# Pools that wait tile by tile, and two pairs of staging tiles for the kept weights, in a two-layer decoder kernel

## The chip, the cores and the metric

The kernel runs on one core of a Trainium2 chip. The metric is the device time of one execution in microseconds (us), as the median of several runs. TensorE is called PE here, VectorE DVE, ScalarE ACT, GpSimd POOL and SyncE SP.

## What is computed

A decoder trunk of two layers on one sequence of 1024 positions with 1024 channels, in float32. Layer 0 mixes by a diagonal state-space model (S5) with a gated output product, layer 1 by stick-breaking attention; each ends with a squared-ReLU MLP of width 4096. Shift, scale and gate of each sub-layer come from a vector c through `ada_w`. Cut to what matters:

```python
for i in range(2):
    sh_a, sc_a, g_a, sh_m, sc_m, g_m = ada_chunks(c, ada_w[i], ada_b[i], 6)
    if i == 0:
        y = s5_mixer(modulate(rms_norm(x, ...), sh_a, sc_a), ...)
        val, gate = split(gelu(y) @ s5_w_glu)
        mix = val * sigmoid(gate)
    else:
        k, v = split(modulate(rms_norm(x, ...), kv_shift, kv_scale) @ w_kv)
        q = modulate(rms_norm(x, ...), sh_a, sc_a) @ sb_w_q
        mix = stick_breaking_attention(norm(q), norm(k), v) @ sb_w_o
    x = x + g_a * mix
    h = modulate(rms_norm(x, ...), sh_m, sc_m)
    x = x + g_m * (square(relu(h @ mlp_w1[i])) @ mlp_w2[i])
```

## The kernel before, in words

**Products.** Every float32 matrix is held as a rounded part and a remainder (`uh` and `ul` for weights, `hi` and `lo` for activations), and `mm3` (L247 to L249) makes three matmuls of one product. A weight unit of 128x1024 is loaded through SP into one of the three `raw` tiles (L208), copied to `uh` by ACT (L214), and DVE makes `ul` by a subtraction (L84; helper lines such as L70, L75, L78, L81, L84 and L93 hold the arithmetic of many places, so the tile names tell which).

**Stages, in us of the profiled execution.** S5 to about 235; the gated product (GLU) to about 400; the MLP of layer 0 to about 1130; the norms of layer 1, then attention from 1145 to 1790; the output projection to 1830; the MLP of layer 1 to the end.

**Side jobs.** Beside GLU and the MLP of layer 0 two kinds of jobs run that prepare later stages. A *gemv* job loads 128 rows of the transposed `ada_w` (512 KB, L173, tile `raw`, through SP, the same three `raw` tiles as the weight units) and reduces them against a row on DVE (L174). A *keep* job works on POOL alone: load 256 KB of `wo`, `wkv` or `wq` into tile `ks` (L227), for `wkv` and `wq` multiply by a scale (L78, `scl`), round into tile `kr` (L232), subtract (L84), and store both to HBM as `kh` and `kl` (L235), so that attention and the output projection later only fetch them (L240). There are 64 keep jobs, 16 for `wo` and 48 for `wkv` and `wq`. `queue` mixes two gemv jobs to one keep job, and `pump`, called from `glu` and from `mid` in the MLP, takes jobs off that list. POOL also adds squares for the norms (L81, tile `f`), which the MLP's norm waits for.

**What sets the order.** S5 has an order written by hand; the rest is put in order by a scheduler when the program is built, and each engine and each DMA queue then issues in that order.

**Tiles and pools.** Pool `adap` has one `ks` and one `kr`, so the next keep load waits until the store of the last one has read `ks`. The class `Inner` gives the tiles `f` (halves of the MLP's hidden activations, work tiles of the norms) in turn from pool "a" (8) and pool "b" (20), and the raw results `ra` and `rb` from "b". A pool opened on bytes of a released pool lets its first instructions wait for every user of what was released. Pools opened late are those of attention (`atp`, `atk`, `atq`, `pz`, `ppt`, `ppo`) and, after it, the pool `x` into which 16 loads bring the residual back from HBM (`x<-xd`, L1611).

```python
raw = adap.tile([P, HN], F32, tag="ks", name=nm("ks"), bufs=1)
hi = adap.tile([P, HN], F32R, tag="kr", name=nm("kr"), bufs=1)
G.dma_start(raw, src[:, cs])
```

Of the kernel before, what the change touches and what calls it, by code (L numbers as in the profile page):

```python
# [8 lines left out]
F32 = mybir.dt.float32  # L9
F32R = mybir.dt.float32r  # L10
# [11 lines left out]
HN = 512  # L22
# [34 lines left out]
def kernel(ctx, tc, A, out):  # L57
# [42 lines left out]
    pools, turns = {}, {}  # L100

    def open_x(i):
        es = ExitStack()
        pools["x"] = es.enter_context(tc.tile_pool(name=f"xp{i}", bufs=16 if i else 1))
        pools["raw"] = es.enter_context(tc.tile_pool(name=f"raw{i}", bufs=3))
        es.callback(pools.pop, "raw")
        turns.clear()
        return es

    def open_ax(i):  # L110
        es = ExitStack()
        pools["ax"] = es.enter_context(tc.tile_pool(name=f"pax{i}", bufs=4 if "pv" in pools else 6, space=PSUM))
        return es

    cnt = [0]
# [13 lines left out]

    def open_pv():  # L130
        es = ExitStack()
        pools["pv"] = es.enter_context(tc.tile_pool(name="ppv", bufs=2, space=PSUM))
        es.callback(pools.pop, "pv")
        return es

# [57 lines left out]
    def queue(jobs, n, others):  # L193
        while jobs or others:
            side.extend(jobs[:n] + others[:1])
            del jobs[:n], others[:1]

    def scale_cols(n, sc0):
        stt(scl[:, 8 * n:8 * n + 8], mod[:, sc0:sc0 + 8], 1.0, gcol[:, 8 * n:8 * n + 8],
            ALU.add, ALU.mult)  # L200
# [15 lines left out]
        return uh, ul  # L216


    kept = {}

    def keep(key, src, c, scale=None):
        if c == 0:
            kept[key] = [dp.tile([P, 1024], F32, name=nm(name)) for name in ("kh", "kl")]
        cs = slice(HN * c, HN * c + HN)
        raw = adap.tile([P, HN], F32, tag="ks", name=nm("ks"), bufs=1)
        hi = adap.tile([P, HN], F32R, tag="kr", name=nm("kr"), bufs=1)
        G.dma_start(raw, src[:, cs])  # L227
        if scale is not None:
            nk = scale.shape[1] // 2
            r3 = raw.rearrange("p (k m) -> p k m", k=nk)  # L230
            mul(r3, r3, scale[:, nk * c:nk * c + nk].unsqueeze(2).broadcast_to([P, nk, HN // nk]), G)
# [25 lines left out]

    def s5(hook):
        es = ExitStack()
        sp = es.enter_context(tc.tile_pool(name="sp", bufs=1))  # L260
        pp = es.enter_context(tc.tile_pool(name="s5ps", bufs=2, space=PSUM))

        cst = sp.tile([P, C_N], F32, name="cst")
        SP.dma_start(cst, A["cst"])
# [70 lines left out]
        dt, mag, th = s("dt"), s("mag"), s("th")  # L335
# [4 lines left out]
        n, r, z = s("e1"), s("e2"), s("e3")  # L340
# [203 lines left out]
        class Block:  # L544
# [165 lines left out]
            pv, vt = None, None  # L710
# [93 lines left out]
    class Norm:  # L804
# [56 lines left out]
    class Inner:  # L861
# [3 lines left out]
            self.n, self.es, self.pools = 0, ExitStack(), {}  # L865

        def open(self, name):
            self.pools[name] = self.es.enter_context(tc.tile_pool(name="fp" + name, bufs=1))

        def tile(self, dt=F32R):  # L870
            a = self.n % 28 < 8
            self.n += 1
            return self.pools["ab"[not a]].tile([P, HN], dt, tag="f", name=nm("f"), bufs=8 if a else 20)

        def raw(self, tag):
            return self.pools["b"].tile([P, HN], F32, tag=tag, name=nm(tag), bufs=2)
# [13 lines left out]
    def mlp(layer, xs, hs, norm, fs, mid=None, done=None):  # L890
        w1, w2 = A["w1"][layer], A["w2"][layer]
        gm = M_GM0 if layer == 0 else M_GM1
        f_tile = fs.tile
        hid, raws = {}, {}
# [7 lines left out]
            mul(r, r, r)  # L902
            return r

        def halves(r):
            hi, lo = f_tile(), f_tile()
            ACT.copy(hi, r)  # L907
            sub(lo, r, hi)
            return hi, lo
# [8 lines left out]
        def enter(j, h, r):  # L918
            raws[j, h] = r
            i = j % 2  # L920
            if (j, h) == (1, 0) or (j, h) == (2, 0):
                hid["B11", i] = halves(raws[i, 0])
            if h == 1 and j >= 2:
                b11, b12, b21, b22 = raws[i, 0], raws[i, 1], raws[j, 0], raws[j, 1]
                hid["B21", i] = halves(b21)
                hid["B22", i] = halves(b22)
                sub(b22, b22, b12)
                hid["T3", i] = halves(b22)
                sub(b12, b12, b11)
                hid["T1", i] = halves(b12)  # L930
                add(b11, b11, b22)
                hid["T2", i] = halves(b11)
                sub(b21, b21, b11)
                hid["T4", i] = halves(b21)

        def blocks(c, op):
            raw = raw_tile()
# [119 lines left out]

    def attention(xn, bias, xd):
        es = ExitStack()
        ap_ = es.enter_context(tc.tile_pool(name="atp", bufs=1))  # L1060
        ak_ = es.enter_context(tc.tile_pool(name="atk", bufs=1))
        aq_ = es.enter_context(tc.tile_pool(name="atq", bufs=1))

        pz = es.enter_context(tc.tile_pool(name="pz", bufs=3, space=PSUM))
        ppt = es.enter_context(tc.tile_pool(name="ppt", bufs=2, space=PSUM))
        ppo = es.enter_context(tc.tile_pool(name="ppo", bufs=1, space=PSUM))
# [382 lines left out]
        return oh, ou[-2:]  # L1449


    pools["un"] = ctx.enter_context(tc.tile_pool(name="unp", bufs=3))
# [4 lines left out]
    rowp = ada_es.enter_context(tc.tile_pool(name="rowp", bufs=1))  # L1457
    silr = rowp.tile([P, D], F32, name="silr")

    def gate(i):  # L1460
# [6 lines left out]
    def hook(i):  # L1467
# [7 lines left out]
        if i == 1:  # L1475
            gate(0)

    ys = s5(hook)
    adap = ada_es.enter_context(tc.tile_pool(name="adap", bufs=1))
    ax_es = open_ax(0)  # L1480
    xs = [[None, None] for _ in range(8)]
    ordered[0] = True
# [3 lines left out]
            SP.dma_start(xs[k][h], A["xT"][k][:, HN * h:HN * h + HN])  # L1486
    ordered[0] = False
    hs = [[None, None] for _ in range(8)]
    fs = Inner()
    fs.open("a")  # L1490
    norm = Norm(norm_tiles(fs), xs, hs, 2, M_SHM0)
    with tc.tile_pool(name="gp", bufs=1) as gp:
        queue(ada_chunk(M_SHM0) + ada_chunk(M_SCM0, lambda: scale_cols(2, M_SCM0)) + ada_chunk(M_GM0), 2,
              [(lambda i=i, c=c: keep(("o", i), A["wo"][i], c)) for i in range(8) for c in range(2)])

        def glu(i, ug, uv, h):
            ps = ps_pv if h == 1 and i <= 5 else ps_mm
# [12 lines left out]
            norm.square(i, h)  # L1510

        for i in range(6):
            ug, uv = first if i == 0 else (load_unit(A["wglu"][8 + i]), load_unit(A["wglu"][i]))
            for h in range(2):
                glu(i, ug, uv, h)
                if i == 0:
                    for c in range(1 + 3 * h, 4 + 4 * h):
                        gate(c)
            if i:
                pump(9)  # L1520
        for h in range(2):
            for i in range(6, 8):
                ug = load_unit(A["wglu"][8 + i])
                uv = load_unit(A["wglu"][i])
                glu(i, ug, uv, h)
            if h == 0:
                norm.rstd(0)
# [83 lines left out]
            SP.dma_start(xs2[k][h], xd[k][h])  # L1611
    fs = Inner()
    ctx.enter_context(fs.es)
    fs.open("a")
    fs.open("b")
    norm2.np_ = norm_tiles(fs)

    def oproj(i, h, mms):
# [114 lines left out]
```

## Time and profile before

| | us |
|---|---|
| median of 3 runs | 2509.57 (2506.57 to 2510.95) |
| profiled execution | 2508.75 |
| its span | 2507.0 |
| PE busy in the span | 2342.5 |
| DVE busy | 1733.1 |
| ACT busy | 941.7 |
| POOL busy | 908.5 |

The profiled execution lies 0.82 us under the median, and 1.75 us of it lie outside the span. PE is the busiest engine, but not in every stage: the time it lacks is spread over S5, GLU, the MLP of layer 0 and the two ends of attention, and each has to be read by itself.

### The profile page before, as it was taken

To read this page: it belongs to the slowest core of one execution; us is meant where nothing else is said; L and a number is where in the kernel's file an instruction comes from. 1 tells how busy PE (TensorE), PEld (TensorE's weight loads), DVE (VectorE), ACT (ScalarE), POOL (GpSimd) and SP (SyncE) were. 2 spreads that over 40 slices of the span, in tenths; PEclk is the share of its full clock that TensorE was granted. 3 is DMA by queue.
4 is the path that set the end of the run, shared out by engine and by line. 5 is a ranking of instruction groups with operands and counts; after the bars stand their busy time and mean duration, and the time that the engine had idled before them with its cause. 6 is when DMAs were issued, how large, how long until landed. Compare 5 with 4: busy or idle time off the path is not lost.

```text
span 2507.0 us, 33262 instructions
## 1 busy us (share of the span) xinstructions
PE 2342.5 (93%) x12536; PEld 1974.6 (79%) x12536; DVE 1733.1 (69%) x2574; ACT 941.7 (38%) x1710; POOL 908.5 (36%) x963
## 2 busy tenths in 40 slices
PE   3888999999999999997899999998999999999998
PEld 2767787878788888886888888886778888888886
DVE  7997547766655655454677877787583767876787
ACT  4753124211222122132566666665351232223221
POOL 4663343244444445223333332343110322342334
PEclk8899999999999999998999999999999999999999
DMA  4325754655655544232111111126721111111112
GB/s 150 88 77 193 259 186 157 213 205 192 204 196 182 193 175 173 94 119 85 59 56 51 56 64 68 62 100 213 248 87 51 34 51 59 59 43 51 56 54 76
DMA packets 105344, 297.08 MB, mean 119 GB/s; under 512 B 13280, under 2 KB 25568, under 8 KB 105184
## 3 DMA queue, kind: packets, MB, share of 16 engines
q1 hardware_dynamic: 87264, 240.42, 27.9%
q0 software_dynamic: 15360, 50.34, 5.6%
q10 hardware_dynamic: 2560, 4.20, 0.8%
q8 instruction: 99, 1.62, 0.3%
q14 instruction: 61, 0.50, 0.1%
HBM read 241.23 MB, written 49.48 MB: 116 GB/s over the span
## 4 chain that ended last, share of the span: by engine, by line
PE 66%; DVE 16%; DMA 9%; issue 4%; ACT 2%; POOL 0%; SPq 0%; DVEq 0%; ACTq 0%; POOLq 0%
PE pm L247 9%; PE pm L248 9%; PE pm L249 9%; PE pm L70 8%; DMA raw<-in_adaT_dram 7%; PE pa L969 3%; PE pa L971 3%; PE pa L970 3%; PE pa L249 3%; PE pa L247 3%; PE pa L248 3%; PE pt L70 3%; DVE sn L1250 3%; PE po L70 2%; PE z L70 2%
## 5 line engine op out<-in xcount | busy, mean ns | idle before, releaser
L247 PE MATMUL pm<-h,uh 128*128 128x512 f32 x1200 | 469.3, 394 | 23.8 <-issue 13.8
L249 PE MATMUL pm<-h,ul 128*128 128x512 f32 x1200 | 469.9, 392 | 4.6 <-DVE ul L84 4.6
L248 PE MATMUL pm<-h,uh 128*128 128x512 f32 x1200 | 471.2, 393 | 1.0 <-DVE h L93 0.9
L214 ACT CAST uh<-raw 128x1024 fp32r<-128x1024 f32 x130 | 136.6, 1051 | 481.8 <-PE pa L248 153.1
L247 PEld LDWEIGHTS pm<-h,uh 128*128 128x128 f32 x1200 | 227.5, 190 | 74.2 <-issue 14.0
L174 DVE CUSTOM_DVE_ANT_0 raw<-raw,silr 128x1024 f32<-128x1024 f32 x119 | 162.1, 1365 | 174.0 <-DMA raw<-in_adaT_dram 160.1
L84 DVE TENSOR_TENSOR ul<-raw,uh 128x1024 fp32r<-128x1024 f32 (+1 forms) x158 | 192.4, 1218 | 124.5 <-ACT uh L214 101.8
L249 PEld LDWEIGHTS pm<-h,ul 128*128 128x128 f32 x1200 | 227.6, 190 | 53.5 <-DVE ul L84 5.9
L248 PEld LDWEIGHTS pm<-h,uh 128*128 128x128 f32 x1200 | 227.6, 190 | 49.5 <-DVE h L93 2.3
L70 PE MATMUL pm<-uh,h 128*128 128x256 f32 x960 | 223.0, 299 | 0.0
L1250 DVE TENSOR_TENSOR_SCAN sn<-sn 128x768 f32<-128x768 f32 (+7 forms) x128 | 180.5, 1416 | 47.3 <-ACT sn L1245 45.9
L81 POOL TENSOR_TENSOR raw<-raw 128x256 f32<-128x256 f32 x28 | 26.0, 927 | 412.3 <-DVE ul L84 412.3
L70 PEld LDWEIGHTS pm<-uh,h 128*128 128x128 f32 x960 | 169.1, 196 | 0.5
L969 PE MATMUL pa<-f,uh 128*128 128x512 f32 x392 | 153.2, 391 | 3.3 <-ACT f L907 2.6
L247 PE MATMUL pa<-f,uh 128*128 128x512 f32 x396 | 154.4, 390 | 0.0
L248 PE MATMUL pa<-f,uh 128*128 128x512 f32 x396 | 154.1, 389 | 0.0
L249 PE MATMUL pa<-f,ul 128*128 128x512 f32 x396 | 153.8, 389 | 0.0
L970 PE MATMUL pa<-f,uh 128*128 128x512 f32 x392 | 153.1, 391 | 0.0
L971 PE MATMUL pa<-f,ul 128*128 128x512 f32 x392 | 145.9, 390 | 0.0
L70 PE MATMUL pm<-ul,h 128*128 128x256 f32 x480 | 137.9, 287 | 0.0
L78 POOL TENSOR_TENSOR sg<-sg,sn 128x512 f32<-128x512 f32 x64 | 92.9, 1452 | 123.5 <-DVE sn L1250 57.4
L78 POOL TENSOR_TENSOR ks<-ks,scl 128x512 f32<-128x512 f32 x48 | 61.2, 1274 | 196.2 <-DMA ks<-in_wkv_dram 96.7
(363 smaller groups left out, 5370.5 us busy)
## 6 DMA issues: line engine op xcount, KB each, us to landing
raw<-in_w_dram SPq DMA_DIRECT2D x140, 512.0 KB, 3.3
raw<-in_adaT_dram SPq DMA_DIRECT2D x96, 512.0 KB, 4.1
uh<-kh SPq DMA_DIRECT2D x40, 512.0 KB, 4.1
ul<-kl SPq DMA_DIRECT2D x40, 512.0 KB, 4.1
kh<-kr POOLq DMA_DIRECT2D x64, 256.0 KB, 2.4
kl<-ks POOLq DMA_DIRECT2D x64, 256.0 KB, 3.1
raw<-in_wT_dram SPq DMA_DIRECT2D x24, 512.0 KB, 4.5
raw<-in_wglu_dram SPq DMA_DIRECT2D x20, 512.0 KB, 4.2
```

The costliest lines, as they stand in the source:

```text
L70: return lambda *a, **k: tc.keep_in_program_order(f(*a, **k))
L78: eng.tensor_tensor(o, a, b, op=ALU.mult)
L84: eng.tensor_tensor(o, a, b, op=ALU.subtract)
L174: V.tensor_tensor_reduce(raw, raw, row, 1.0, 0.0, op0=ALU.mult, op1=ALU.add, accum_out=bcol)
L214: ACT.copy(uh, raw)
L247: T.matmul(ps, uh[:, sl], hi, start=first, stop=False)
L248: T.matmul(ps, uh[:, sl], lo, start=False, stop=False)
L249: T.matmul(ps, ul[:, sl], hi, start=False, stop=last)
L969: T.matmul(p, uh[:, sl], hi, start=(i == 0), stop=False)
L970: T.matmul(p, uh[:, sl], lo, start=False, stop=False)
L971: T.matmul(p, ul[:, sl], hi, start=False, stop=(i == 1))
L1250: V.tensor_tensor_scan(g[:, s0:], g[:, s0:], g[:, s0:], 1.0, op0=ALU.mult, op1=ALU.bypass)
```

## The change

1. All pools that are opened on released bytes are opened with `reuse_waits="tile"`: an instruction on a new tile waits for the users of those old tiles whose bytes it overlays, and not for all users of the old pool.
2. `adap` is gone. `keep` takes its tiles from a new pool "e" of `Inner`: four of its eight tiles, two pairs, of which the first serves the left half of a weight and the second the right half. Successive keep jobs thus use different tiles.
3. `Inner`'s pool "a" has 20 `f` tiles, "e" has 8, and "b" only `ra` and `rb`. In layer 1 the halves (`wide=True`) go round all 28 as before; in layer 0 all `f` tiles go round the 20 of "a".

```diff
+    def tile_pool(name, bufs=1, **k):
+        return tc.tile_pool(name=name, bufs=bufs, reuse_waits="tile", **k)
...
-        pools["x"] = es.enter_context(tc.tile_pool(name=f"xp{i}", bufs=16 if i else 1))
-        pools["raw"] = es.enter_context(tc.tile_pool(name=f"raw{i}", bufs=3))
+        pools["x"] = es.enter_context(tile_pool(f"xp{i}", bufs=16 if i else 1))
+        pools["raw"] = es.enter_context(tile_pool(f"raw{i}", bufs=3))
...
-        raw = adap.tile([P, HN], F32, tag="ks", name=nm("ks"), bufs=1)
-        hi = adap.tile([P, HN], F32R, tag="kr", name=nm("kr"), bufs=1)
+        while len(keeps) < 4:
+            keeps.append(fs0.extra((F32, F32R)[len(keeps) % 2]))
+        raw, hi = keeps[0:2] if c == 0 else keeps[2:4]
...
-        def tile(self, dt=F32R):
-            a = self.n % 28 < 8
-            self.n += 1
-            return self.pools["ab"[not a]].tile([P, HN], dt, tag="f", name=nm("f"), bufs=8 if a else 20)
+        def tile(self, dt=F32R, wide=False):
+            self.n += wide
+            if wide and (self.n - 1) % 28 >= 20:
+                return self.extra(dt)
+            return self.pools["a"].tile([P, HN], dt, tag="f", name=nm("f"), bufs=20)
+
+        def extra(self, dt):
+            return self.pools["e"].tile([P, HN], dt, tag="e", name=nm("e"), bufs=8)
...
-        ap_ = es.enter_context(tc.tile_pool(name="atp", bufs=1))
-        ak_ = es.enter_context(tc.tile_pool(name="atk", bufs=1))
-        aq_ = es.enter_context(tc.tile_pool(name="atq", bufs=1))
+        ap_ = es.enter_context(tile_pool("atp", bufs=1))
+        ak_ = es.enter_context(tile_pool("atk", bufs=1))
+        aq_ = es.enter_context(tile_pool("atq", bufs=1))
...
-    adap = ada_es.enter_context(tc.tile_pool(name="adap", bufs=1))
...
-    fs = Inner()
+    fs = fs0 = Inner()
     fs.open("a")
+    fs.open("e")
```

Both programs have the same number of instructions on every engine. In the rows below a name's number tells tiles of the same kind apart only where it is needed.

**POOL in the MLP of layer 0**, in its steady run of keep jobs on `wkv`; before (a load, L227, stands behind both stores of the job ahead of it):

```order
L227 DMA ks_5373<-in_wkv_dram 128x512
L78 TENSOR_TENSOR ks_5373<-ks_5373,scl 128x512
L232 CAST kr_5374<-ks_5373 128x512
L84 TENSOR_TENSOR ks_5373<-ks_5373,kr_5374 128x512
L235 DMA kh_5295<-kr_5374 128x512
L235 DMA kl_5296<-ks_5373 128x512
L227 DMA ks_5451<-in_wkv_dram 128x512
L78 TENSOR_TENSOR ks_5451<-ks_5451,scl 128x512
L232 CAST kr_5452<-ks_5451 128x512
L84 TENSOR_TENSOR ks_5451<-ks_5451,kr_5452 128x512
```


and now (`e_2492` with `e_2493` is one pair, `e_2494` with `e_2495` the other; the keep load is L231, the rounding L236, the stores L239):

```order
L239 DMA kl_5248<-e_2492 128x512
L78 TENSOR_TENSOR e_2494<-e_2494,scl 128x512
L236 CAST e_2495<-e_2494 128x512
L231 DMA e_2492<-in_wkv_dram 128x512
L84 TENSOR_TENSOR e_2494<-e_2494,e_2495 128x512
L239 DMA kh_5247<-e_2495 128x512
L239 DMA kl_5248<-e_2494 128x512
L78 TENSOR_TENSOR e_2492<-e_2492,scl 128x512
L236 CAST e_2493<-e_2492 128x512
L231 DMA e_2494<-in_wkv_dram 128x512
```


The load of the next job has moved ahead of the subtraction and the two stores of the job in work.

**POOL at the start of GLU**, up to the first sum of squares for the norm (the L81 row); before:

```order
L70 TENSOR_TENSOR h_2119<-xall,h_2118 128x512
L227 DMA ks_2492<-in_wo_dram 128x512
L70 TENSOR_TENSOR h_2182<-xall,h_2181 128x512
L70 TENSOR_TENSOR h_2186<-xall,h_2185 128x512
L232 CAST kr_2493<-ks_2492 128x512
L84 TENSOR_TENSOR ks_2492<-ks_2492,kr_2493 128x512
L235 DMA kh_2490<-kr_2493 128x512
L235 DMA kl_2491<-ks_2492 128x512
L227 DMA ks_2505<-in_wo_dram 128x512
L232 CAST kr_2506<-ks_2505 128x512
L84 TENSOR_TENSOR ks_2505<-ks_2505,kr_2506 128x512
L235 DMA kh_2490<-kr_2506 128x512
L81 TENSOR_TENSOR f_2273<-f_2273,f_2425 128x512
```


and now:

```order
L70 TENSOR_TENSOR h_2119<-xall,h_2118 128x512
L231 DMA e_2492<-in_wo_dram 128x512
L70 TENSOR_TENSOR h_2182<-xall,h_2181 128x512
L70 TENSOR_TENSOR h_2186<-xall,h_2185 128x512
L236 CAST e_2493<-e_2492 128x512
L231 DMA e_2494<-in_wo_dram 128x512
L84 TENSOR_TENSOR e_2492<-e_2492,e_2493 128x512
L239 DMA kh_2490<-e_2493 128x512
L239 DMA kl_2491<-e_2492 128x512
L236 CAST e_2495<-e_2494 128x512
L84 TENSOR_TENSOR e_2494<-e_2494,e_2495 128x512
L239 DMA kh_2490<-e_2495 128x512
L239 DMA kl_2491<-e_2494 128x512
L231 DMA e_2492<-in_wo_dram 128x512
L231 DMA e_2494<-in_wo_dram 128x512
L81 TENSOR_TENSOR f_2273<-f_2273,f_2425 128x512
```


Four keep loads stand ahead of the first sum of squares where two stood.

**SP at the end of attention**, with what each row waits for (semaphores by engine, `DMAHW` for a queue); before:

```order
L240 DMA ul_16359<-kl_2821 128x1024 [waits DMAHW0_49,PE_49]
L1345 DMA xd_1_3530<-kn_16131 128x512 [waits DMAHW1_49,DVE_49]
L1611 DMA x_16371<-xd_0_3525 128x512 [waits DVE_49,DMAHW2_49,PE_49,Pool_49]
L1611 DMA x_16373<-xd_0_3527 128x512 [waits DMAHW3_49]
L1611 DMA x_16375<-xd_0_3529 128x512 [waits DMAHW4_49]
```


and now:

```order
L244 DMA ul_16235<-kl_2813 128x1024 [waits DMAHW0_49,PE_49]
L1353 DMA xd_1_3502<-kn_16007 128x512 [waits DMAHW1_49,DVE_49]
L1619 DMA x_16247<-xd_0_3497 128x512 [waits DMAHW2_49,Activation_49]
L1619 DMA x_16249<-xd_0_3499 128x512 [waits DMAHW3_49]
L1619 DMA x_16251<-xd_0_3501 128x512 [waits DMAHW4_49,Pool_49]
```


The order is the same; the first `x<-xd` load no longer waits for DVE, PE and POOL, but for ACT.

## Rows read from the trace of the kernel before

**Rows 1.** The page: span, busy time of the engines, the chain that ended last by engine.

```profile
span 2507.0 us, 33262 instructions
...
PE 2342.5 (93%) x12536; PEld 1974.6 (79%) x12536; DVE 1733.1 (69%) x2574; ACT 941.7 (38%) x1710; POOL 908.5 (36%) x963
...
PE 66%; DVE 16%; DMA 9%; issue 4%; ACT 2%; POOL 0%; SPq 0%; DVEq 0%; ACTq 0%; POOLq 0%
```

**Rows 2.** PE, PEld, DVE, ACT, POOL busy us (count) by stretch; clock, DMA share, GB/s.

```profile
242.00:262.00 20.00, 20.00 (x90) 16.52 (x89) 7.51 (x11) 3.57 (x7) 2.93 (x4) 1.00 0.98 356
254.00:324.00 70.00, 64.99 (x270) 52.21 (x270) 38.70 (x53) 12.52 (x17) 22.81 (x23) 0.95 0.71 249
473.00:637.00 164.00, 160.07 (x692) 131.17 (x691) 102.19 (x138) 27.63 (x38) 74.56 (x80) 0.98 0.59 208
800.00:1030.00 230.00, 230.00 (x1033) 191.02 (x1032) 129.79 (x154) 49.96 (x69) 106.88 (x121) 1.00 0.49 171
```

**Rows 3.** The chain in 448 to 640 us: start us, us, what.

```profile
by line: DMA raw<-in_adaT_dram 59.4%; DVE raw L174 15.3%; issue 9.6%; DVE ul L84 8.1%; DVE xall L93 5.1%; DVE ra L78 1.1%; DVE mod L174 0.8%; DVE f L84 0.5%; DVEq L174 0.2%; DVE mod L81 0.1%; DVE scl L93 0.1%; DVEq L84 0.0%
...
456.96 4.52 DMA raw<-in_adaT_dram
...
532.94 4.91 DMA raw<-in_adaT_dram
...
558.01 5.58 DMA raw<-in_adaT_dram
...
584.32 5.22 DMA raw<-in_adaT_dram
```

**Rows 4.** POOL in order of time, one keep job: start us, us, what [idle <-releaser].

```profile
563.04 1.03 POOL L78 TENSOR_TENSOR ks<-ks,scl 128x512 f32<-128x512 f32 x1 [5.02 <-DMA ks<-in_wkv_dram]
564.14 1.49 POOL L232 CAST kr<-ks 128x512 fp32r<-128x512 f32 x1
565.71 1.61 POOL L84 TENSOR_TENSOR ks<-ks,kr 128x512 f32<-128x512 f32 x1
567.27 0.58 POOL L235 DMA_DIRECT2D kh<-kr  x1
567.85 0.54 POOL L235 DMA_DIRECT2D kl<-ks  x1
571.25 0.54 POOL L227 DMA_DIRECT2D ks<-in_wkv_dram  x1 [2.86 <-DMA kl<-ks]
```

**Rows 5.** Tile ks by line: ns min/median/max, first and last start us.

```profile
L78 POOL TENSOR_TENSOR ks<-ks,scl x48: 1034/1037/2093, 473.5 to 1028.8; 128x512 f32<-128x512 f32 x48
```

**Rows 6.** DVE in order of time in 525 to 532 us.

```profile
527.15 1.74 DVE L78 TENSOR_TENSOR rb<-rb 128x512 f32<-128x512 f32 x1
529.58 0.69 DVE L84 TENSOR_TENSOR f<-rb,f 128x512 fp32r<-128x512 f32 x1 [0.68 <-ACT f L907]
```

**Rows 7.** What PE waited for: total us, times, longest us.

```profile
PE pm L247 <- issue: 13.8, 1, 13.8
PE pm L247 <- ACT rb L901: 7.5, 3, 3.6
PE pm L249 <- DVE ul L84: 4.6, 3, 3.7
PE pa L247 <- DVE x L93: 1.8, 1, 1.8
PE pa L249 <- DMA ul<-kl: 0.5, 1, 0.5
```

**Rows 8.** DVE in order of time, 1156 to 1160 us.

```profile
1156.33 1.46 DVE L75 TENSOR_TENSOR h<-f,h 128x512 fp32r<-128x512 f32 x2
1157.89 0.43 DVE L81 TENSOR_TENSOR kn<-pm,brow 128x256 f32<-128x256 f32 x1
```

**Rows 9.** SP in order of time at the end of attention.

```profile
1787.59 0.32 SPq L1345 DMA_DIRECT2D xd<-kn  x1
1790.02 9.79 SPq L1611 DMA_DIRECT2D x<-xd  x16
```

More of the change, by code (lines that the diff above doesn't have):

```diff
@@ L111, in open_ax @@
         es = ExitStack()
-        pools["ax"] = es.enter_context(tc.tile_pool(name=f"pax{i}", bufs=4 if "pv" in pools else 6, space=PSUM))
+        pools["ax"] = es.enter_context(tile_pool(f"pax{i}", bufs=4 if "pv" in pools else 6, space=PSUM))
         return es
@@ L131, in open_pv @@
         es = ExitStack()
-        pools["pv"] = es.enter_context(tc.tile_pool(name="ppv", bufs=2, space=PSUM))
+        pools["pv"] = es.enter_context(tile_pool("ppv", bufs=2, space=PSUM))
         es.callback(pools.pop, "pv")
@@ L216, in split_unit @@
         return uh, ul
-    kept = {}
+    kept, keeps = {}, []
     def keep(key, src, c, scale=None):
@@ L259, in s5 @@
         es = ExitStack()
-        sp = es.enter_context(tc.tile_pool(name="sp", bufs=1))
-        pp = es.enter_context(tc.tile_pool(name="s5ps", bufs=2, space=PSUM))
+        sp = es.enter_context(tile_pool("sp", bufs=1))
+        pp = es.enter_context(tile_pool("s5ps", bufs=2, space=PSUM))
         cst = sp.tile([P, C_N], F32, name="cst")
@@ L867, in open @@
         def open(self, name):
-            self.pools[name] = self.es.enter_context(tc.tile_pool(name="fp" + name, bufs=1))
-        def tile(self, dt=F32R):
-            a = self.n % 28 < 8
-            self.n += 1
-            return self.pools["ab"[not a]].tile([P, HN], dt, tag="f", name=nm("f"), bufs=8 if a else 20)
+            self.pools[name] = self.es.enter_context(tile_pool("fp" + name))
+        def tile(self, dt=F32R, wide=False):
[5 more added lines that the diff above has]
+            return self.pools["e"].tile([P, HN], dt, tag="e", name=nm("e"), bufs=8)
         def raw(self, tag):
@@ L903, in up, with halves @@
             return r
-        def halves(r):
-            hi, lo = f_tile(), f_tile()
+        def halves(r, wide=False):
+            hi, lo = f_tile(wide=wide), f_tile(wide=wide)
             ACT.copy(hi, r)
@@ L921, in enter @@
             if (j, h) == (1, 0) or (j, h) == (2, 0):
-                hid["B11", i] = halves(raws[i, 0])
+                hid["B11", i] = halves(raws[i, 0], True)
             if h == 1 and j >= 2:
                 b11, b12, b21, b22 = raws[i, 0], raws[i, 1], raws[j, 0], raws[j, 1]
-                hid["B21", i] = halves(b21)
-                hid["B22", i] = halves(b22)
+                hid["B21", i] = halves(b21, True)
+                hid["B22", i] = halves(b22, True)
                 sub(b22, b22, b12)
-                hid["T3", i] = halves(b22)
+                hid["T3", i] = halves(b22, True)
                 sub(b12, b12, b11)
-                hid["T1", i] = halves(b12)
+                hid["T1", i] = halves(b12, True)
                 add(b11, b11, b22)
-                hid["T2", i] = halves(b11)
+                hid["T2", i] = halves(b11, True)
                 sub(b21, b21, b11)
-                hid["T4", i] = halves(b21)
+                hid["T4", i] = halves(b21, True)
         def blocks(c, op):
@@ L1059, in attention @@
         es = ExitStack()
-        ap_ = es.enter_context(tc.tile_pool(name="atp", bufs=1))
-        ak_ = es.enter_context(tc.tile_pool(name="atk", bufs=1))
-        aq_ = es.enter_context(tc.tile_pool(name="atq", bufs=1))
-        pz = es.enter_context(tc.tile_pool(name="pz", bufs=3, space=PSUM))
-        ppt = es.enter_context(tc.tile_pool(name="ppt", bufs=2, space=PSUM))
-        ppo = es.enter_context(tc.tile_pool(name="ppo", bufs=1, space=PSUM))
+        ap_ = es.enter_context(tile_pool("atp", bufs=1))
+        ak_ = es.enter_context(tile_pool("atk", bufs=1))
+        aq_ = es.enter_context(tile_pool("atq", bufs=1))
+        pz = es.enter_context(tile_pool("pz", bufs=3, space=PSUM))
+        ppt = es.enter_context(tile_pool("ppt", bufs=2, space=PSUM))
+        ppo = es.enter_context(tile_pool("ppo", bufs=1, space=PSUM))
         klz = [[[ak_.tile([P, HN], F32R, name=f"klz_{i}_{h}_{a}") for a in range(2)] for h in range(2)]
@@ L1449, in attention @@
         return oh, ou[-2:]
-    pools["un"] = ctx.enter_context(tc.tile_pool(name="unp", bufs=3))
+    pools["un"] = ctx.enter_context(tile_pool("unp", bufs=3))
     x_es = open_x(0)
@@ L1456 @@
     ada_es = ExitStack()
-    rowp = ada_es.enter_context(tc.tile_pool(name="rowp", bufs=1))
+    rowp = ada_es.enter_context(tile_pool("rowp", bufs=1))
     silr = rowp.tile([P, D], F32, name="silr")
@@ L1488 @@
     hs = [[None, None] for _ in range(8)]
-    fs = Inner()
+    fs = fs0 = Inner()
     fs.open("a")
+    fs.open("e")
     norm = Norm(norm_tiles(fs), xs, hs, 2, M_SHM0)
-    with tc.tile_pool(name="gp", bufs=1) as gp:
+    with tile_pool("gp", bufs=1) as gp:
         queue(ada_chunk(M_SHM0) + ada_chunk(M_SCM0, lambda: scale_cols(2, M_SCM0)) + ada_chunk(M_GM0), 2,
@@ L1613 @@
     ctx.enter_context(fs.es)
-    fs.open("a")
-    fs.open("b")
+    for name in "aeb":
+        fs.open(name)
     norm2.np_ = norm_tiles(fs)
```

## Prediction

> **What bounds the kernel now.** I read the page first, for the share of each engine on the chain that ended last; then the table by stretch, because an average over stages says nothing about one; then the chain inside the stretches where PE is not alone; and last the waits at the places that the change touches.
>
> The page shows PE on 66% of the chain, DVE on 16%, DMA on 9% and POOL on none of it [rows 1]. So nothing that makes POOL faster can pay by itself; it acts through the transfers that it issues, earlier or later. The stretches differ [rows 2]. From 800 to 1030 us PE is busy all the time: there a transfer that is late by a microsecond, or gone, changes nothing. From 254 to 324 PE is busy 64.99 of 70 us, and from 473 to 637 160.07 of 164. In these two PE's lack is the end of another chain: from 448 to 640 us, 59.4% of the chain is the load of a gemv job and 15.3% its reduction on DVE [rows 3]. A gemv load needs a free `raw` tile, which the reduction frees, and the reduction needs the load. PE stands in none of these pieces, so each microsecond that such loads grow there moves what follows by a microsecond. The reader is to see in the rows that the loads on this chain are not alike: 4.52 us at 456.96, before the keep jobs on `wkv` begin, and 4.91 to 5.58 us for five later ones with a keep load under them, three of which are shown.
>
> What the change works on is the keep job. POOL's own work for one is 1.03, 1.49, 1.61, 0.58 and 0.54 us, and 0.54 to issue the load: 5.8 us. Besides that it waits 5.02 us for the load and 2.86 us for the store that frees `ks` [rows 4]. The 48 scaled jobs start between 473.5 and 1028.8 us [rows 5], one per 555.3 / 47 = 11.8 us.
>
> **Part 1, the end of attention.** SP issues the last store at 1787.59 and the first `x<-xd` load at 1790.02, although their queue is the same [rows 9]; in the order above the second no longer waits for DVE, PE and POOL but for an ACT result. It can follow the store, some 2.1 us earlier (1790.02 less 1787.59 and 0.32). The 16 loads take 9.79 us together and PE then stalls 1.8 us for `x` and 0.5 for a `ul` fetch [rows 7]. I take 1.8 off; the bounds are 0 (the loads find their engines busy) and 2.3. A loss has no source here: the same transfers go in the same order.
>
> **Part 2, the start of attention.** PE has its longest wait there, 13.8 us [rows 7]. The wait on the released pools is gone from the first `kn` addition, but that addition stands in DVE's order behind two `h<-f,h` that run from 1156.33 to 1157.79, and begins at 1157.89 [rows 8]. DVE issues in order and its order there is unchanged, so it begins no earlier than 1157.79: at most 0.1 us. I take 0.
>
> **Part 3, GLU.** Four keep loads stand ahead of the first sum of squares in place of two, and the first need not wait for S5's last tiles. Two loads of 0.262 MB more, and one store of 0.262 MB that stood behind it, come earlier. From 242 to 262 us DMA is 98% busy at 356 GB/s [rows 2]; there 3 x 0.262 MB take 2.2 us, and the weight unit that the chain waits for behind them comes later by that. Over the rest of the stage I count two further jobs brought forward into the chain, at the price of part 4, 0.9 each. That is +4.0. The lower bound is -0.4 (nothing grows, and the `ul` that PE waits for comes a little earlier by a changed DVE order), the upper one five jobs of 0.786 MB at 356 GB/s, 2.2 us each: 11.
>
> **Part 4, the MLP of layer 0.** With two pairs the load is issued ahead of the subtraction and the stores of the job before, so POOL waits neither for the store nor for most of the load. The period falls from 11.8 us towards the 5.8 us of POOL's own work; I take 8, since POOL also has the sums of squares and weight blocks, and loads slow each other. In the 167 us from 473 to 640 that makes 21 jobs where there were 14: 7 more. The 48 jobs end at about 473 + 48 x 8 = 857 us and not 1030, but what is freed after 857 lies where PE is busy all the time, and buys nothing. The price of one more job: the three loads shown have a mean of 5.24 us, 0.72 above the 4.52 without a keep load [rows 3]. Beside POOL's work DVE can be slower too: a square of `rb` took 1.74 us at 527.15, where a subtraction of that size took 0.69 [rows 6], 1.05 more; I count it for one job in six, 0.18. So 0.9 a job, 7 x 0.9 = +6.3. The lower bound is 0 (the stretch has room: DMA is 59% busy [rows 2]); the upper is the full bytes, 7 x 2.2 = 15.4.
>
> For this bound there is a rule. The Trainium skill (DMA: Bandwidth & Descriptors, section "Issuing engines are not separate DMA queues") says that transfers started by sync or gpsimd run on the same 16 DMA engines and interleave, whoever started them. By it, the keep transfers that POOL starts earlier take their time from the gemv loads that SP starts, and the upper bound would hold where the engines are full; the loads of rows 3 grew by a third of that.
>
> **Part 5, costs of nothing.** In layer 0 the `f` tiles go round 20 and not 28. A half written over an older tile follows an up product that stands behind the down products which read the old tile in PE's order, so it waits for nothing new. In layer 1 the round is 28 as before. S5's end, the scores and the MLP of layer 1 keep their order and their bounds; earlier memsets of attention's tiles on POOL feed nothing that PE waits for.
>
> **Sum.** -1.8 + 0 + 4.0 + 6.3 = +8.5. The profiled execution took 2508.75 us, 0.8 under the median of the runs. 2508.75 + 8.5 = 2517.3; I say **2517**.
>
> **The rivals.**
>
> *Faster: the chains have slack for the transfers, and the waits alone count.* If the loads do not grow, because DMA is only 59% and 71% busy in the two stretches, part 1 gives up to 2.3 and the `ul` stalls of 4.6 us in three places [rows 7] go with the changed DVE order and the earlier keep jobs: 2508.75 - 6.9 = 2501.9. It decides if an additional keep load costs the chain less than 0.1 us. For it: PE lost only 7.5 us to late `rb` results in the kernel [rows 7]. Against: the rows 3 difference.
>
> *No change: covered.* The loads grow as in rows 3 but the growth is met by fewer collisions later, while PE still has work in hand; only part 1 is left: 2507, or up to 2512 with part 3 alone (2508.75 - 1.8 + 4 = 2511).
>
> *Heavy: full price.* Extra bytes take their full time from the chain in both stages: -1.8 + 11 + 15.4 = +24.6, 2533. For it: 98% busy DMA at 242. Against: rows 3. This is what the skill's rule gives.
>
> *The gap closes.* If DVE's order in execution let `kn` begin when PE's first tile is ready, 13.8 us go beside 1.8 or more: 2508.75 - 15.6 = 2493. Against: the order is fixed.
>
> *The change does not do what it says*: keep jobs stay serial because POOL waits for loads anyway, or because other work between them sets the pace. That ends as "covered", near 2509, and is counted there.
>
> **How the numbers follow.** A measurement of this kernel can tell about 0.2% from no change, 5.0 us: below 2504.6 is faster, above 2514.6 slower. My forecast has 0.45, 0.09 of it under 2514.6; covered 0.25; faster 0.13; heavy 0.13; the closed gap 0.04. Faster is 0.13 + 0.04 and 0.01 from the edge of covered, 0.18; same 0.24 + 0.09 = 0.33; slower 0.36 + 0.13 = 0.49. The range runs from 2502, the faster rival, to 2531, just under the heavy one; it leaves out the closed gap, two thirds of heavy, and half of faster's lower edge, together about 0.18.
>
> **What would show it.** Right: keep jobs on `wkv` every 7 to 9 us and their end near 860; gemv loads on the chain between 473 and 640 us at 5 to 6 us, and more PE stall on `ra` or `rb` there, about 6 us; the first `x<-xd` load right behind the store with PE's wait for `x` gone; the wait of 13.8 us still there. Wrong: loads of the chain unchanged with jobs at 8 us (faster or covered); chain loads of 6.5 us or more (heavy); a period still near 12 us (the change does not act); a new wait of ACT or PE on `f` tiles in layer 0, which part 5 excludes.

## The result and the profile after

The change makes the kernel slower. The median of six runs is 2523.03 us (2518.38 to 2533.55), that of six runs of the kernel before 2506.26 us (2505.39 to 2510.95); the ratio is 1.0069, with a 95% interval of 1.0049 to 1.0089. That is +16.8 us by the medians, in the range and on the side that was forecast, and twice the sum of +8.5. The profiled execution of the changed kernel took 2528.77 us; it is the second slowest of the six and lies 5.7 above their median, as that of the kernel before, 2508.75, lies 2.5 above its own. The two traces are thus 20.0 us apart where the medians are 16.8, and what follows is read from them.

The page of the changed kernel:

```profile
span 2527.0 us, 33256 instructions
...
PE 2343.6 (93%) x12536; PEld 1971.4 (78%) x12536; DVE 1751.3 (69%) x2574; ACT 941.6 (37%) x1710; POOL 902.0 (36%) x963
...
PE 62%; DVE 17%; DMA 10%; issue 6%; ACT 2%; POOL 1%; DVEq 0%; SPq 0%; POOLq 0%; ACTq 0%
```

PE works as long as before [rows 1], DVE 18.2 us longer, though no instruction was added to either. The table by stretch of the changed kernel, columns as in [rows 2]:

```profile
254.00:324.00 70.00, 64.84 (x273) 52.77 (x272) 36.52 (x51) 10.14 (x15) 30.23 (x35) 0.95 0.79 276
473.00:637.00 164.00, 153.23 (x653) 124.26 (x653) 110.13 (x132) 25.56 (x35) 126.11 (x143) 0.97 0.72 251
650.00:780.00 130.00, 118.09 (x502) 96.24 (x503) 95.23 (x96) 24.97 (x36) 103.63 (x122) 0.95 0.71 243
800.00:1030.00 230.00, 230.00 (x1032) 191.03 (x1031) 115.34 (x161) 50.52 (x71) 0.00 (x0) 1.00 0.33 112
```

and the one stretch of the kernel before that was not among the rows read ahead:

```profile
650.00:780.00 130.00, 130.00 (x575) 107.63 (x575) 78.52 (x105) 23.46 (x32) 59.52 (x69) 1.00 0.58 200
```

In GLU (254 to 324) PE is as busy as before although DMA moves more. Between 473 and 637 PE loses 10.8 us instead of 3.9, POOL's work has gone from 74.56 to 126.11 us, and DVE is busy longer with fewer instructions (110.13 us for 132 against 102.19 for 138). Between 650 and 780 PE was never idle before, and now lacks 11.9 us. After 800 POOL does nothing and PE is full in both kernels. The waits of PE in the changed kernel (answering to [rows 7]):

```profile
PE pm L251 <- ACT rb L909: 22.9, 7, 7.4
PE pm L251 <- issue: 13.6, 1, 13.6
PE pm L253 <- DVE ul L84: 5.2, 2, 4.3
PE pa L251 <- DMA uh<-kh: 2.8, 1, 2.8
PE pa L251 <- DVE xall L93: 1.8, 1, 1.8
```

The wait for `rb` (PE waits until ACT has emptied an earlier result into it) has grown by 15.4 us, one of 1.8 us for `xall` is new, and the one before attention's first projection stands. The keep jobs' scaling (answering to [rows 5]):

```profile
L78 POOL TENSOR_TENSOR e<-e,scl x48: 1035/1118/2090, 473.5 to 788.2; 128x512 f32<-128x512 f32 x48
```

The 48 jobs start in 314.7 us instead of 555.3, one per 6.7 us. At the end of attention, SP in order of time (answering to [rows 9]):

```profile
1808.16 0.32 SPq L1353 DMA_DIRECT2D xd<-kn  x1
1808.57 11.72 SPq L1619 DMA_DIRECT2D x<-xd  x16
```

Placed by the same PE instruction in both traces, the changed execution is 1.5 us late at the start (a load that the change doesn't touch), 0.2 us late at the 2500th (464.89 us against 464.71), 22.6 us late at the 4000th (840.37 against 817.79), and 20.0 late at the 12500th. So the whole loss arises in the MLP of layer 0, before about 785 us. No engine waits for POOL between 473 and 800 us in either trace, so other work that might be late behind the denser jobs on POOL is not the cause.

### The profile page after: what moved, and what is told of

It reads as the page before. It is cut to its first block, busy times and chain, and to the rows that moved or that the text cites. A ratio compares the mean times of both kernels' runs of the same rounds, so it can differ in the third digit from the quotient of the medians.

```text
span 2527.0 us, 33256 instructions
## 1 busy us (share of the span) xinstructions
PE 2343.6 (93%) x12536; PEld 1971.4 (78%) x12536; DVE 1751.3 (69%) x2574; ACT 941.6 (37%) x1710; POOL 902.0 (36%) x963
## 4 chain that ended last, share of the span: by engine, by line
PE 62%; DVE 17%; DMA 10%; issue 6%; ACT 2%; POOL 1%; DVEq 0%; SPq 0%; POOLq 0%; ACTq 0%
PE pm L251 8%; PE pm L253 8%; PE pm L252 8%; PE pm L70 8%; DMA raw<-in_adaT_dram 8%; PE pa L977 3%; PE pa L979 3%; PE pa L978 3%; DVE sn L1258 3%; PE pt L70 2%; PE pa L251 2%; PE pa L252 2%; PE pa L253 2%; PE po L70 2%; PE z L70 2%
## 5 line engine op out<-in xcount | busy, mean ns | idle before, releaser
L251 PE MATMUL pm<-h,uh 128*128 128x512 f32 x1200 | 470.4, 395 | 39.6 <-ACT rb L909 22.9
L252 PE MATMUL pm<-h,uh 128*128 128x512 f32 x1200 | 471.3, 393 | 0.0
L84 DVE TENSOR_TENSOR ul<-raw,uh 128x1024 fp32r<-128x1024 f32 (+1 forms) x158 | 199.9, 1265 | 125.8 <-ACT uh L217 103.2
L177 DVE CUSTOM_DVE_ANT_0 raw<-raw,silr 128x1024 f32<-128x1024 f32 x119 | 170.0, 1433 | 163.8 <-DMA raw<-in_adaT_dram 149.5
L81 POOL TENSOR_TENSOR f<-f,f 128x512 f32<-128x512 f32 x36 | 50.6, 1406 | 423.4 <-ACT f L825 402.8
L81 POOL TENSOR_TENSOR raw<-raw 128x256 f32<-128x256 f32 x28 | 26.0, 929 | 412.3 <-DVE ul L84 412.3
L251 PE MATMUL pa<-f,uh 128*128 128x512 f32 x396 | 154.9, 391 | 1.8 <-DVE xall L93 1.8
L252 PE MATMUL pa<-f,uh 128*128 128x512 f32 x396 | 154.7, 391 | 0.0
L253 PE MATMUL pa<-f,ul 128*128 128x512 f32 x396 | 154.5, 391 | 0.0
L93 DVE SCALAR_TENSOR_TENSOR x<-pa,mod,x 128x512 f32<-128x512 f32 x143 | 103.4, 742 | 40.4 <-PE pa L253 33.4
L1253 ACT ACTIVATE sn<-z,rrr 128x512 f32<-128x512 f32 (+1 forms) x192 | 111.5, 581 | 47.9 <-PE z L70 45.4
L70 PE MATMUL pm<-h,uh 128*128 128x512 f32 x386 | 127.9, 412 | 0.0
```

Of the source, the lines that this page charges most:

```text
L70: return lambda *a, **k: tc.keep_in_program_order(f(*a, **k))
L177: V.tensor_tensor_reduce(raw, raw, row, 1.0, 0.0, op0=ALU.mult, op1=ALU.add, accum_out=bcol)
L251: T.matmul(ps, uh[:, sl], hi, start=first, stop=False)
L252: T.matmul(ps, uh[:, sl], lo, start=False, stop=False)
L253: T.matmul(ps, ul[:, sl], hi, start=False, stop=last)
L1253: ACT.activation(g[:, HN * hb + c0:HN * hb + HN], p[:, c0:], AF.Sigmoid, scale=pj.rr[:, 2, t, a:a + 1])
```

## The experiments

Two theories stood after this. **A**: POOL's arithmetic, now denser, slows DVE. **B**: the transfers, now denser, lengthen the gemv loads, as part 4 had it. A rival, **C**: the 20 `f` tiles or the new pool waits. Ratios are to the kernel before, in runs on the same chip, with 95% intervals.

**One pair, serial again.**

```diff
-        raw, hi = keeps[0:2] if c == 0 else keeps[2:4]
+        raw, hi = keeps[0:2]
```

> The changed kernel, but every keep job uses the same one pair of tiles, so that jobs are serial again; pools wait tile by tile and layer 0 goes round 20 f tiles, as in the change. If the loss comes from denser keep jobs (theory A: their POOL arithmetic makes DVE slower; theory B: their transfers make gemv loads longer), the time falls back to 2503 to 2508 us, the jobs on wkv start 11 to 12 us apart and PE's waits for rb return to about 7.5 us. If it comes from the 20 f tiles or from the new pool waits (theory C), the time stays at 2519 to 2527 us.

Measured: 1.0003 (0.9990 to 1.0017), 2515.03 us against 2513.94 on this chip.

PE's wait for `rb`, and the scaling of the keep jobs by line:

```profile
PE pm L251 <- ACT rb L909: 9.0, 2, 4.6
```
```profile
L78 POOL TENSOR_TENSOR e<-e,scl x48: 1034/1036/1981, 476.6 to 1034.4; 128x512 f32<-128x512 f32 x48
```

Serial jobs, one per 11.9 us, and the loss is gone, with the 20 tiles and the tile-by-tile waits in place. These two, and with them part 1's gain, are worth nothing that can be measured; C falls. (The expected time was put for another chip; the ratio decides.)

**Two pairs, pools that wait for all users.**

```diff
-        return tc.tile_pool(name=name, bufs=bufs, reuse_waits="tile", **k)
+        return tc.tile_pool(name=name, bufs=bufs, **k)
```

> The changed kernel with two pairs, but pools opened on released bytes wait for all users, as before. A and B: the loss stays, 2519 to 2527 us, since the dense keep jobs stay; the first x load at the end of attention stands about 2 us after the store again. C (pool waits are the loss): 2503 to 2509 us.

Measured: 1.0080 (1.0056 to 1.0103). The two pairs alone make the loss.

**Transfers whole, arithmetic of the keep jobs on one column in 32.** (The scaling is cut in the same way.)

```diff
...
-        G.tensor_copy(hi, raw)
-        sub(raw, raw, hi, G)
+        G.tensor_copy(hi[:, 0:16], raw[:, 0:16])
+        sub(raw[:, 0:16], raw[:, 0:16], hi[:, 0:16], G)
```

> The changed kernel with the keep jobs' transfers whole, but scaling, rounding and subtraction done on 16 columns of 512 (of 4 in each 128 when scaled), the rest left out, so that the transfers come even closer together and POOL does almost no arithmetic. A: no loss, 2500 to 2508 us, a gemv reduction (L177) in 473 to 700 us has a mean of 1.2 to 1.3 us. B: a loss at least like the change's, 2521 us or more, with gemv loads longer than the 3.9 us of both kernels there.

Measured: 1.0041 (1.0025 to 1.0056). Neither theory had this: bytes alone cost, but less than the change, although jobs came every 5.9 us.

**Arithmetic whole, almost no bytes.**

```diff
-        G.dma_start(raw, src[:, cs])
+        G.dma_start(raw[:, 0:16], src[:, HN * c:HN * c + 16])
...
+                G.dma_start(dp.tile([P, 16], F32, name=nm("spare")), t[:, 0:16])
```

> The changed kernel with the keep jobs' arithmetic whole, but load and stores of only 16 columns of 512 (the first key's stores are whole, and all keys then read that one), the rest left out, so that POOL's arithmetic comes as close or closer and almost no bytes move. A: the loss stays, 2516 to 2530 us, and a gemv reduction (L177) has a mean of 1.5 us or more while the jobs run. B: no loss, 2500 to 2508 us.

Measured: 1.0002 (0.9989 to 1.0014), with jobs 7.1 us apart. So A, as the only cause, falls too: DVE is as slow as in the change (below), yet the time is that of before. Both may cost, and this run may have won by having no bytes what it lost by denser arithmetic. That needs the two other corners of a table.

**No keep jobs on `wkv` and `wq`.**

```diff
+        if key[0] != "o":
+            return
```

> The changed kernel without the 48 keep jobs on wkv and wq (attention fetches the first wo weight in their place). Theory A+B, by a sum that fits the four kernels run so far (jobs as dense as the change's cost arithmetic and bytes about the same and add up): POOL arithmetic and bytes both lengthen the chain of load and reduction even in the kernel before, so this is faster than before, ratio 0.991 to 0.996, PE's waits for rb near 0. Rival: the chain is at its floor in the kernel before and only jobs denser than there cost something: ratio 0.998 to 1.000, waits for rb near 7 us.

Measured: 0.9930 (0.9912 to 0.9949). The keep jobs cost 0.7% in the kernel before already.

**Transfers whole, paced.**

```diff
...
+        for _ in range(12 if scale is not None else 8):
+            G.tensor_copy(hi[:, 0:16], raw[:, 0:16])
```

> The changed kernel with whole transfers in the keep jobs and arithmetic on 16 columns only, as in the run with transfers alone, but with the rounding repeated 12 times on these columns, so that jobs start about as far apart as in the change (6 to 7.5 us). A+B additive: the change's ratio of 1.007 to 1.008, less what arithmetic alone adds over no keep jobs, so 0.998 to 1.003. B alone, bytes as the whole cause: 1.006 or more. Gemv loads (L173 before) between 4.0 and 4.4 us in 473 to 700, reductions 1.25 to 1.35.

Measured: 1.0013 (0.9997 to 1.0029); the jobs were 8.6 us apart, slower than wanted.

The four corners are then 0.9930 (nothing), 1.0002 (arithmetic), 1.0013 (bytes), and 1.0069 or, without the tile-by-tile waits, 1.0080 (both). Each ratio is known to between 0.13 and 0.23%. Alone, arithmetic adds 0.72% and bytes add 0.83%; both together add 1.39 to 1.50%, near the sum of 1.55%. So each costs something by itself, and about the same at these distances, which are 6.7 to 8.6 us and not equal: the run with bytes alone and jobs 5.9 us apart stands 1.11% over no keep jobs, so that at the change's 6.7 us bytes alone would cost about 1.0% (an estimate from the two runs). How the change's own cost divides does not follow from the corners. The "nothing" and single corners leave out part of the keep jobs' work (the single ones also in the 16 jobs on `wo` in GLU), so only their times count. The trace shows where each acts. DVE between 473 and 700 us, by line (count, busy us, mean ns, idle before); first the kernel before, with the additions to `xall`, one of whose inputs, `pa`, lies in PSUM:

```profile
L174 DVE CUSTOM_DVE_ANT_0 raw<-raw,silr 128x1024 f32<-128x1024 f32 x42 | 58.0, 1382 | 77.0 <-DMA raw<-in_adaT_dram 77.0
L84 DVE TENSOR_TENSOR ul<-raw,uh 128x1024 fp32r<-128x1024 f32 x20 | 25.8, 1292 | 0.0
L93 DVE SCALAR_TENSOR_TENSOR xall<-pa,mod,xall 128x512 f32<-128x512 f32 x31 | 22.6, 743 | 0.0
```

the change:

```profile
L177 DVE CUSTOM_DVE_ANT_0 raw<-raw,silr 128x1024 f32<-128x1024 f32 x39 | 60.5, 1552 | 67.4 <-DMA raw<-in_adaT_dram 67.4
L84 DVE TENSOR_TENSOR ul<-raw,uh 128x1024 fp32r<-128x1024 f32 x19 | 30.1, 1582 | 0.0
L93 DVE SCALAR_TENSOR_TENSOR xall<-pa,mod,xall 128x512 f32<-128x512 f32 x27 | 19.9, 741 | 0.0
```

arithmetic alone:

```profile
L177 DVE CUSTOM_DVE_ANT_0 raw<-raw,silr 128x1024 f32<-128x1024 f32 x40 | 62.5, 1564 | 55.7 <-DMA raw<-in_adaT_dram 55.7
L84 DVE TENSOR_TENSOR ul<-raw,uh 128x1024 fp32r<-128x1024 f32 x18 | 29.1, 1615 | 0.0
```

bytes alone, paced:

```profile
L177 DVE CUSTOM_DVE_ANT_0 raw<-raw,silr 128x1024 f32<-128x1024 f32 x39 | 48.0, 1230 | 97.0 <-DMA raw<-in_adaT_dram 97.0
```

no keep jobs:

```profile
L177 DVE CUSTOM_DVE_ANT_0 raw<-raw,silr 128x1024 f32<-128x1024 f32 x43 | 52.7, 1225 | 87.1 <-DMA raw<-in_adaT_dram 87.1
```

And the gemv loads of the same stretch (count, size of one, median us to landing). Before:

```profile
raw<-in_adaT_dram SPq DMA_DIRECT2D x40, 512.0 KB, 3.6
```

the change:

```profile
raw<-in_adaT_dram SPq DMA_DIRECT2D x38, 512.0 KB, 3.8
```

arithmetic alone:

```profile
raw<-in_adaT_dram SPq DMA_DIRECT2D x39, 512.0 KB, 3.4
```

bytes alone, paced:

```profile
raw<-in_adaT_dram SPq DMA_DIRECT2D x39, 512.0 KB, 4.5
```

no keep jobs:

```profile
raw<-in_adaT_dram SPq DMA_DIRECT2D x42, 512.0 KB, 3.5
```

A reduction takes 1.225 us with no keep jobs and 1.230 beside bytes alone, but 1.564 beside arithmetic alone and 1.552 in the change. A load takes 3.5 us with no keep jobs and 3.4 beside arithmetic alone, but 4.5 beside bytes alone. Between before and the change a reduction grows by 0.17 and a `ul` subtraction by 0.29, a load's median by 0.2 and its mean by 0.1 (3.90 to 4.01). Over the whole time of the jobs, 473 to 790 us, the mean of the loads is 3.92 us before and 3.94 in the change, 3.81 with no keep jobs, 3.63 beside arithmetic alone and 4.43 beside bytes alone. What DVE waited for between 473 and 800 us says the same; before:

```profile
DVE raw L174 <- DMA raw<-in_adaT_dram: 108.9, 51, 4.4
```

the change:

```profile
DVE raw L177 <- DMA raw<-in_adaT_dram: 94.2, 46, 4.8
```

DVE waits less for gemv loads in the change, 2.05 us each time instead of 2.14, and ACT, which has to empty PE's next result into `rb`, waits longer for DVE's squares of the last one; before:

```profile
ACT f L907 <- DVE rb L78: 61.4, 14, 11.7
```

the change:

```profile
ACT f L915 <- DVE rb L78: 82.3, 12, 15.2
```

So what grew on the way from before to the change is mostly DVE's own work. Beside the denser arithmetic alone the loads became shorter (3.63 us); beside both they did not, and this is what the rows leave for the bytes.

**Late keep jobs.** If they cost only while the chain of gemv loads bounds the stage, they belong behind it. Two pairs make that possible: 48 jobs at 6.7 us fit into 320 us. The keep jobs on `wkv` and `wq` are taken off the common list, the first load of each pair is tied to a gemv result (`TIE` is the number of its column in `mod`; column 80 is done near 700 us), and two jobs are issued per step of the MLP from there; the computation is whole.

```diff
+            G.tensor_copy(raw[:, 0:1], mod[:, TIE:TIE + 1])
         G.dma_start(raw, src[:, cs])
...
-        pump((3, 4)[cyc[0] % 2])
+        pump((3, 4)[cyc[0] % 2] if cyc[0] <= 5 else (2, 2, 3)[cyc[0] % 3])
+        for _ in range(min(2, len(late)) if ready else 0):
+            late.pop(0)()
```

> The changed kernel, whole computation, with the 48 keep jobs on wkv and wq held back until the gemv of column 80 is done (near 700 us), then two per step of the MLP. If what costs is that the jobs run while the chain of gemv loads bounds the stage, this beats both kernels: ratio to before 0.992 to 0.998, no keep job between 440 and 690 us, PE's waits for rb under 4 us. If keep jobs cost wherever they stand (PE or DVE late after 700 us as well), 1.000 to 1.006.

> As the last, but held back until the gemv of column 95, the last of the adaT loads (near 780 us). If the chain is over only then, this is faster than the last by 0.1 to 0.3%, ratio to before 0.990 to 0.997. Against it: 48 jobs at 6.5 us end near 1090 us, and the norm's sums of squares on POOL stand behind them, so if they are late PE waits before attention and the ratio is 1.000 or more.

Column 80 gave 0.9946 (0.9928 to 0.9964), column 95 gave 1.0015 (0.9998 to 1.0032). (On the chips of these runs the kernel before has medians of 2514 to 2518 us, and its trace is an execution of 2508.75; leads over it are therefore rough.) In the trace of column 95 PE is 13.7 us ahead of before at its 3500th instruction, and behind it at attention: the last jobs run on POOL until 1170 us among the norms' work, and PE's long wait before the first projection grows; that wait, and the scaling of the jobs:

```profile
PE pm L257 <- issue: 18.7, 1, 18.7
```
```profile
L78 POOL TENSOR_TENSOR e<-e,scl x48: 1030/1040/2037, 771.7 to 1162.5; 128x512 f32<-128x512 f32 x48
```

> As the run held back to column 80, but to column 72, some 45 us earlier (near 640 us), so that seven or so jobs more run while the chain of gemv loads still bounds. If each of them costs as in the 2x2 of arithmetic and bytes, the ratio to before is 0.996 to 0.999, between the run of column 80 (0.9946) and the change (1.0069).

> As the run held back to column 80, but to column 88 (near 730 us). The chain stage gains some 2 us more; the 48 jobs end near 1070 us, and the norm's sums of squares on POOL begin to stand behind them. If they are still in time, 0.992 to 0.995; if they are late as in the run of column 95, 0.996 to 1.001.

Both gave 1.0004 (0.9990 to 1.0018). Column 72 is a miss; column 88 came out at the time of its second branch, but only in part for the reason given there. It is ahead of before by 14.9 us at the 3500th instruction and loses it after 817 us: 8.8 by the 4500th (929 us), PE being busy 224.36 of 230 us between 800 and 1030, and 8.3 between the 5000th and the 6000th, at the norms and the start of attention, the last scaling starting at 1121. Column 72 lies behind column 80 from 700 us on, PE being busy 91.01 of 100 us up to 800. Why 45 us of start make 0.6% there was not settled. A gain that its neighbours lacked had to be repeated:

> The kernel held back to column 80 once more, since its neighbours at columns 72 and 88 are both at 1.0004: if its gain is its own and not that of a few runs, the ratio to before is again 0.993 to 0.997; if not, 0.998 to 1.001.

Measured: 0.9961 (0.9944 to 0.9978), on another chip. The gain of column 80 is repeated; its neighbours were run on one chip only, a third one. Its table by stretch, columns as in [rows 2]:

```profile
448.00:700.00 252.00, 252.00 (x1113) 208.64 (x1113) 151.62 (x226) 49.54 (x70) 10.08 (x14) 1.00 0.50 160
700.00:800.00 100.00, 95.86 (x412) 77.54 (x411) 62.83 (x76) 19.29 (x29) 62.94 (x77) 0.98 0.67 227
800.00:1030.00 230.00, 226.65 (x1009) 187.72 (x1009) 138.90 (x151) 49.12 (x68) 171.16 (x200) 0.99 0.63 216
```

and that of before:

```profile
448.00:700.00 252.00, 244.48 (x1056) 200.58 (x1055) 161.94 (x219) 46.60 (x64) 102.82 (x113) 0.98 0.61 209
700.00:800.00 100.00, 100.00 (x443) 82.81 (x442) 58.52 (x80) 20.43 (x29) 43.68 (x51) 1.00 0.56 196
```

PE is full from 448 to 700 us, where before it lacked 7.5; it gives 3.4 to 4.1 us back in each of the next two stretches, under the jobs. That is 7.5 in all: this execution, of 2508.40 us, has no gain on the trace of before. The first run's, of 2503.81 us, has one:

```profile
448.00:700.00 252.00, 251.35 (x1109) 208.14 (x1110) 153.12 (x228) 52.05 (x73) 10.69 (x16) 1.00 0.50 164
700.00:800.00 100.00, 99.86 (x441) 82.38 (x440) 67.01 (x78) 21.01 (x31) 67.31 (x81) 1.00 0.67 224
800.00:1030.00 230.00, 226.46 (x1010) 187.63 (x1009) 139.38 (x152) 47.03 (x65) 163.26 (x194) 0.99 0.63 215
```

PE lacks 0.65, 0.14 and 3.54 us there. So the gain at column 80 is shown by the times of two sets of runs; that it comes of PE being full up to 700 us is read from single executions, and columns 88 and 95 are full there too without a gain.

> The same, with the rounding of the 48 late jobs on ACT and not on POOL. If POOL's arithmetic beside DVE is what the wait for rb near 884 us comes from, this wait shrinks and jobs come closer together: 0.991 to 0.995. If ACT's queue makes PE wait, because the rounding stands there ahead of weight copies until POOL has scaled, 0.996 to 1.003.

```diff
-        G.tensor_copy(hi, raw)
+        (ACT.copy if scale is not None else G.tensor_copy)(hi, raw)
```

Measured: 1.0061 (1.0039 to 1.0083), a miss in size. The rounding now stands in ACT's order ahead of weight copies and halves and waits there until POOL has scaled; what ACT waited for between 650 and 1130 us:

```profile
ACT e L242 <- POOL e L78: 140.6, 39, 10.8
```

and PE in the same run:

```profile
PE pm L257 <- ACT rb L915: 14.6, 4, 5.0
```

## Why the prediction was right in sign and short in size

**Part 4, the mis-sized term.** +6.3 us were forecast, and the stretch from the 2500th to the 4000th PE instruction gave +22.4. Three things were in the term.

- *The number of jobs.* The prediction saw that "what is freed after 857 lies where PE is busy all the time", but what was brought forward was counted only to 640 us, because PE was full in the kernel before from 650 on. It was full there with 11.8 us between jobs; with 6.7 the chain is the bound up to the end of the `adaT` loads near 780, and PE lacks 11.9 us (its row of 650 to 780 above). Up to 640 us 25 jobs started where 14 had and 21 were forecast, and from 473 to 788 all 48 ran where 27 would have: 21 more, not 7. At the forecast price of 0.9 that alone is 18.9. This is the step that failed: a stage with no idle time was taken for one with slack.
- *The price's parts.* 0.72 for a longer load and 0.18 for DVE. The 22.4 us over 21 jobs are 1.07 per job, so their sum was near, but by luck, for its parts were not. The sign that was named for being right, gemv loads of 5 to 6 us on the chain, did not come: of the loads issued between 473 and 790 us, 4 of 51 took 5 us or more in the change and 5 of 54 before, and their mean is as good as the same. Unchanged loads beside a shorter period had been named as a sign of being wrong, and the time rose all the same, through DVE. The 0.72 came from three loads that were chosen because a keep load ran beside them, set against one of 4.52; all 30 issued between 473 and 640 us before have a mean of 3.92. On DVE it is not one job in six: the reductions and the `ul` subtractions grew in the mean of the whole stretch, and a square of `rb`, of which the row of 1.74 us [rows 6] was one, takes 1.08 us in the kernel before and 1.05 in the change, but 0.69 with no keep jobs.
- *PE's clock.* It was left out. After each long wait PE ran slower for some time: the granted clock is 0.50 from 536 to 542 us, around the end, at 538.46, of a wait of 7.12 us. From 700 to 800 us the granted clock is 0.97 where it was 1.00 (0.97 being a mean of time at 2.4 and at 1.2 GHz), and 398 matmuls take 92.98 us (0.234 each) where 443 took 100.00 (0.226). With 448 to 700 that is some 5 of the 22.4 us, worked out from

```profile
448.00:700.00 252.00, 233.87 (x1002) 190.54 (x1001) 172.04 (x206) 44.55 (x63) 173.19 (x199) 0.97 0.71 244
700.00:800.00 100.00, 92.98 (x398) 75.18 (x397) 68.34 (x74) 17.77 (x25) 74.28 (x88) 0.97 0.69 238
...
536.00:542.00 6.00, 3.54 (x8) 2.81 (x9) 3.48 (x3) 2.06 (x3) 4.91 (x6) 0.50 0.57 197
```

With the 15.4 us of longer waits for `rb` and the new 1.8 for `xall` these 5 make up the 22.4.

**Part 3** was forecast at +4.0; in the profiled execution some 1.3 us came back up to the 2500th PE instruction. DMA's share from 254 to 324 rose from 0.71 to 0.79, and three of PE's stalls in GLU grew by 1.4, so the loads brought forward cost something there, but less than forecast; a stall of 0.35 in GLU and two just behind it (413 to 422 us), 2.2 together, went.

**Part 1** did what it said, and its time did not come. The first `x<-xd` load is issued 0.41 us behind the store, and the wait for `x` is gone; but the 16 issues now take 11.72 us instead of 9.79 [rows 9] and end 12.1 us behind the store where they ended 12.2 behind it, the weight fetch after them is hardly earlier, and PE waits 2.8 us for `uh<-kh`, where it waited 1.8 for `x`. 1.8 were taken off, 0.4 came between the 9250th and the 9750th instruction, near the lower bound of 0. That its reason ("the loads find their engines busy") is why the issues took longer is not shown.

**Part 2 and part 5** were right: 13.6 us of wait for 13.8, and the run with one pair shows that 20 tiles cost nothing that can be measured.

**The rivals.** "Covered" and "faster" fell; "heavy", at +24.6 us, is about as near to the measured 16.8 as the forecast, but its mechanism is not what was found: the loads did not take the full time of the extra bytes from the chain, and arithmetic without bytes costs 0.72% over no keep jobs. By the Trainium skill's rule that part 4 quotes (DMA: Bandwidth & Descriptors), alone, the loss would have stayed whole in the run with bytes, and the run with arithmetic would have come down to the 0.9930 of no keep jobs; they stand at 1.0013 (1.0041 with jobs 5.9 us apart) and 1.0002.

## What to carry to other kernels

Before a background job is made faster, find out which stretch it will then run in and what is in balance there: an engine that is busy all the time next to a second chain with no slack is not a cushion. Double-buffering work that nothing waits for only moves its contention forward. Here it paid (0.9946 and 0.9961) at one of four points to which the jobs were held back, and not at its neighbours, so such a point has to be searched for. A table of four runs (nothing, arithmetic alone, bytes alone, both) shows that two causes share a cost where single-cause theories each fail; how it divides has to be read in the trace of the kernel with both.

## What the runs showed of the hardware

POOL's arithmetic on SBUF tiles slows DVE and not the DMA loads, and transfers slow loads and not DVE: reductions of 1.225 us became 1.564 beside POOL's arithmetic and stayed at 1.230 beside bytes; loads of 3.5 us (median) stayed at 3.4 beside arithmetic and became 4.5 beside bytes. The additions to `xall`, with one input in PSUM, stayed at 0.74 us in all of these. The Trainium skill (SBUF — State Buffer, section "SBUF: two separate sides") says that the engines' side and the DMA side of SBUF don't contend, and that on the engines' side only a pair of ports that DVE and GpSimd share does; these rows agree with it. Part 4 had put 0.72 of its 0.9 us on the loads and 0.18 on DVE, and it was mostly DVE's work that grew.
